# Shifting the on-chip addresses of the normalised activations by 32 bytes and of every other tile by 256 bytes

## The chip, the core and the metric

The kernel runs on one core of one Trainium2 chip. The metric is the device time of one launch in microseconds, as the median of three runs. "PE" is TensorE, "DVE" VectorE, "ACT" ScalarE, "POOL" GpSimd and "SP" SyncE, which issues the DMAs. SBUF is the on-chip memory of 128 partitions; an address below is a byte offset within a partition.

## The reference, cut to what matters

One sequence of 256 tokens with 1024 features goes through two layers of a first block and one layer of a second. Each layer multiplies normalised activations by large weight matrices:

```python
for l in range(2):                                  # first block
    h = rmsnorm(x, norm_mix[l])
    proj = h @ w_in[l]                              # 1024 x 5956
    ...
    x = x + merged @ w_out[l]
    h = rmsnorm(x, norm_ffn[l])
    g, u = jnp.split(h @ w_ffn_in[l], 2, axis=-1)   # 1024 x 5632
    x = x + (jax.nn.silu(g) * u) @ w_ffn_out[l]     # 2816 x 1024
...                                                 # second block: the same shape of work, once
h = rms_norm(x, mix_pre_g) * (1.0 + sc1) + sh1
y = hybrid_mixer(h, w_in, ...)
x = x + g1 * rms_norm(y, mix_post_g)
h = rms_norm(x, ffn_pre_g) * (1.0 + sc2) + sh2
y = swiglu_ffn(h, w_ffn_in, w_ffn_out)
```

All of it is float32.

## The kernel before, in words

**How a product is made.** Each float32 operand is split into a rounded part H and a remainder L (both of type fp32r), and a product is the sum of three matmuls, H·H, H·L and L·H (`mm3`, line 776). Weights come from HBM in 350 tiles of 128 partitions x 1024 columns (tag `raw`, 4 buffers); ACT writes the H half (`wH`) and DVE the L half (`wL`), 6 buffers each (`do_split`, line 716). The normalised activations of a stage are split in the same way into two tiles of 128 x 8 x 256, `xH` and `xL`, made by `act_pair` (line 868).

**What PE does with them.** Before each matmul, a load of weights (the profile's engine row PEld) brings a 128 x 128 block into the array; then the other operand, the moving one, streams through. In a name such as `mm<-xH,wL`, the first operand is the moving one and the second the loaded one. There are five kinds of fp32r matmul:

- `pair_mm` (line 781): moving `xH` or `xL`, 256 columns; loaded `wH` or `wL`. Called for the input projections, the gates and both halves of the first FFN product (`ffn`, lines 1360 and 1362).
- `proj_mm` (line 790): moving a `b4` tile (name `b` in the profile), 256 columns.
- `out_mm` (line 890): moving a `t512` tile (`t`) or an `E` tile, 256 columns.
- `token_mm` (line 799) and `first_tm` (line 1326): moving `wH` or `wL`, 512 columns; loaded `xH` or `xL`.
- `out_tm` (line 902): moving `wH` or `wL`, 512 columns; loaded `xH` and `xL` (where `act_pair` holds the mixer's output, line 1630) or a `t512` tile.

**What sets the order.** All instructions are recorded first (`Recorder`, line 346; the profile therefore gives nearly every instruction line 396) and then issued in an order that a list scheduler works out from fixed costs per instruction. The costs depend on shapes and engines, not on addresses.

**Where tiles lie.** `new` (line 640) makes tiles of a multiple of 128 bytes per partition, and the pools hand out addresses in the order in which tags are first used. In the built program `raw`, `wH`, `wL`, `xH`, `xL` and all `b4` tiles start at 256 bytes past a multiple of 512. All `t512` and `E` tiles start at 384 bytes past one. The slices that a matmul reads inside these tiles are 512, 1024 or 2048 bytes long and lie at multiples of 512 bytes from the tile's start, except slices of the two small weight tiles (68 and 8 columns).

Of the kernel before, what the change touches and what calls it, by code (L numbers as in the profile page):

```python
# [16 lines left out]
F32R = mybir.dt.float32r  # L17
# [9 lines left out]
LAST = 0.0  # L27
FF, NJ = 2816, 11
LINE = 128
OUT_SHAPE = [256, 1024]  # L30
EPS = 1e-6
NEG = -1e30
# [583 lines left out]
def program(tc, I, out, pw, cw, tap=None, stop=None):  # L616
# [11 lines left out]
    with es:  # L628
        es.enter_context(tc.manual_schedule())
        const = es.enter_context(tc.tile_pool(name="const", bufs=1))  # L630
        wp = es.enter_context(tc.tile_pool(name="wp", bufs=3))
        act = es.enter_context(tc.tile_pool(name="act", bufs=1))
# [4 lines left out]
        def body():  # L637
            uid = [0]

            def new(pool, shape, dt=F32, tag=None, bufs=None):  # L640
                n = int(np.prod(shape[1:]))
                line = LINE if dt == U8 else LINE // 4
                if pool is not psum and pool is not dram and n % line:

                    v = new(pool, [shape[0], -(-n // line) * line], dt, tag, bufs)[:, :n]
                    return v if len(shape) == 2 else v.rearrange("p (a b) -> p a b", a=shape[1])
                uid[0] += 1
                b = Buf(pool, shape, dt, f"{tag or 'c'}_{uid[0]}", tag, bufs or 1, "PSUM" if pool is psum else "SBUF")
                return View(b, np.arange(n).reshape([1] + list(shape[1:])), shape[0], ())
# [98 lines left out]
            DMA.dma_start(cst[:, :early], I["consts"][:, :early])  # L748
            DMA.dma_start(cst[:, early:], I["consts"][:, early:])
            msk = new(const, [128, 5, 32], U8)  # L750

            def load_masks():
                m = b4()[:, :160]
                DMA.dma_start(m, I["masks"])
                V.tensor_copy(msk.rearrange("p a b -> p (a b)"), m)
# [110 lines left out]
                return v, r, rstd  # L866

            def act_pair():
                return (new(act, [128, 8, 256], F32R, tag="xH", bufs=1), new(act, [128, 8, 256], F32R, tag="xL", bufs=1))

            def scaled_split(g, acc=None):

                H, L = act_pair()
                for c in range(8):
                    if acc is not None and c % 2 == 0:
                        tt(x2(c // 2), x2(c // 2), acc[c // 2], OP.add)
                    A(H[:, c], xT[:, c], AF.Copy, scale=g[:, c:c + 1])
                    stt(L[:, c], xT[:, c], g[:, c:c + 1], H[:, c].bitcast(F32), OP.mult, OP.subtract)
                return H, L
# [575 lines left out]
            for i, n in enumerate(("mix", "ffn")):  # L1455
                a = new(const, [128, 8])
                stt(a, mod[f"sc{i + 1}"], 1.0, P(f"{n}_pre_g"), OP.add, OP.mult)
                b = new(const, [128, 8])
# [3 lines left out]
            def modulated(n):  # L1462
                g, _, sh, _ = G[n]
                rstd = rstd_of(squares(x2), 1024, "side", True)[2]
                H, L = act_pair()
                for p in range(4):
                    t = t512()
                    tt(v2(t), xT[:, 2 * p:2 * p + 2], bc(rstd, 2), OP.mult)
                    for b in range(2):
                        c = 2 * p + b  # L1470
                        s = slice(b * 256, b * 256 + 256)
                        if c in MOD_V:
                            ts(t[:, s], t[:, s], g[:, c:c + 1], sh[:, c:c + 1], OP.mult, OP.add)
                        else:
                            A(t[:, s], t[:, s], AF.Identity, scale=g[:, c:c + 1], bias=sh[:, c:c + 1])
                    w = lambda ap: ap[:, 2 * p:2 * p + 2].rearrange("p a b -> p (a b)")
                    split_into(w(H), w(L), t)
                return H, L
# [39 lines left out]
            def modulated_tm(n):  # L1518
                g, _, sh, _ = G[n]
                H, L = act_pair()  # L1520
                first = first_tm()
                for t in range(2):
                    R.bias = EARLY if t == 0 else 0.0
                    r = inv_rms(lambda h: xt[:, t, h * 512:h * 512 + 512])
                    for h in range(2):
                        z, m, ps = t512(), t512(), bank()
                        ts(z, xt[:, t, h * 512:h * 512 + 512], r, 32.0, OP.mult, OP.mult)
                        for i in range(4):
                            PE.transpose(ps[:, i * 128:i * 128 + 128], z[:, i * 128:i * 128 + 128], ident)
                        for i in range(4):  # L1530
                            c = 4 * h + i
                            sl = slice(i * 128, i * 128 + 128)
                            if i < ON_V[h]:
                                ts(m[:, sl], ps[:, sl], g[:, c:c + 1], sh[:, c:c + 1], OP.mult, OP.add)
                            else:
                                A(m[:, sl], ps[:, sl], AF.Identity, scale=g[:, c:c + 1], bias=sh[:, c:c + 1])
                        w = lambda ap: ap[:, 4 * h:4 * h + 4, t * 128:t * 128 + 128]
                        split_into(w(H), w(L), m.rearrange("p (a b) -> p a b", a=4))
                    R.bias = 0.0
                    pend = first(t, H, L)  # L1540
                return (H, L), pend
# [4 lines left out]
            for tag, n in (("iq", 16), ("AT1", 16), ("cr", 8), ("sr", 8), ("qnc", 8), ("qns", 8), ("knc", 8), ("kns", 8)):  # L1546
                n = min(n, 16 * GROUPS - len(taps))
                if n > 0:
                    t = new(act, [128, n, 32], F32, tag=tag)
# [137 lines left out]
            post("ffn", ffn(X, None, None, out_tm, first), True)  # L1687

        body()
        R.issue()  # L1690
        tc.predicted = R.predicted
# [16 lines left out]
```

## Time and profile before

| | |
|---|---|
| median of 3 runs | 1154.72 us (1154.36 to 1154.79) |
| the profiled execution | 1152.33 us |
| its span, first to last instruction | 1150.6 us |
| PE busy | 1120.6 us (97%), 9388 matmuls |
| DVE busy | 857.8 us (75%) |
| ACT busy | 595.1 us (52%) |
| DMA queue of the weights | 55.6% of 16 engines' time |
| mean granted TensorE clock | 0.995 of full speed |

The span is 1.7 us shorter than the device time of the same execution, and that execution is 2.4 us (0.2%) below the median. A matmul's busy time in the profile is its latency, so the busy times of neighbours overlap; what one matmul costs in a stream is the distance from its start to the next start. The chain of waits gives that for whole streams: its pieces state how long a run of consecutive matmuls held the end of the program, and how many there were.

### The profile page before, as it was taken

The page shows a single profiled execution, that of the slowest core. Times are in us where ns is not written, and L with a number is a line of the kernel's source. Part 1 is how long each engine was busy: PE and PEld are TensorE (multiplying, and loading weights), DVE is VectorE, ACT ScalarE, POOL GpSimd, SP SyncE. Part 2 cuts the span into 40 slices and gives each one's busy share as a digit, 9 for nine tenths or more (in the row PEclk, how much of TensorE's full clock was granted, in tenths as well). Part 3 has the DMA queues.
Part 4 walks back from the last instruction along what each step waited for, and adds up shares of the span by engine and source line. Part 5 has one row for each costly group of instructions (what it writes and reads, how often), then busy time and mean ns, then how long its engine had stood idle before and what let it go on. Part 6 is the DMA issues. An engine that isn't in the chain of part 4 may idle for free.

```text
span 1150.6 us, 22970 instructions
## 1 busy us (share of the span) xinstructions
PE 1120.6 (97%) x9388; PEld 1060.2 (92%) x9388; DVE 857.8 (75%) x1590; ACT 595.1 (52%) x905; POOL 7.2 (1%) x16
## 2 busy tenths in 40 slices
PE   6999999999999999999999999999899989999996
PEld 6989999999999999888999999999799568999995
DVE  7999976889965589998676998755879668444554
ACT  6745594544444467446745544444654665443442
POOL 1000000000000000000000000000000000000000
PEclk9999999999999999999999999999999999999999
DMA  7553544788956543644355898656456325556550
GB/s 268 173 188 107 185 131 155 245 283 327 334 170 216 185 146 113 218 133 135 133 177 189 287 347 310 209 195 194 137 173 182 107 74 196 169 177 209 184 165 36
DMA packets 59992, 217.47 MB, mean 189 GB/s; under 512 B 6872, under 2 KB 10096, under 8 KB 56816
## 3 DMA queue, kind: packets, MB, share of 16 engines
q1 hardware_dynamic: 59888, 216.02, 55.6%
q8 instruction: 73, 1.20, 0.4%
q14 instruction: 31, 0.25, 0.1%
HBM read 214.19 MB, written 1.63 MB: 188 GB/s over the span
## 4 chain that ended last, share of the span: by engine, by line
PE 95%; DVE 2%; ACT 1%; issue 1%; DMA 0%; SPq 0%; DVEq 0%; ACTq 0%
PE mm L396 66%; PE side L396 29%; DVE small L396 1%; DVE b L396 1%; DVE wL L396 0%; DMA raw<-in_W 0%; ACT t L396 0%; ACT wH L396 0%; DVE t L396 0%; DVE xL L396 0%; SPq L396 0%; DVE E L396 0%; DVE c L396 0%; DVE AC L396 0%; DVEq L1704 0%
## 5 line engine op out<-in xcount | busy, mean ns | idle before, releaser
L396 ACT ACTIVATE wH<-raw 128x1024 fp32r<-128x1024 f32 (+1 forms) x390 | 368.6, 967 | 420.6 <-PE mm L396 227.0
L396 DVE TENSOR_TENSOR wL<-raw,wH 128x1024 fp32r<-128x1024 f32 (+1 forms) x390 | 425.0, 1110 | 163.6 <-ACT wH L396 162.0
L396 PE MATMUL mm<-xH,wH 128*128 128x256 f32 x1760 | 497.0, 285 | 9.2 <-ACT wH L396 9.2
L396 PE MATMUL mm<-xL,wH 128*128 128x256 f32 x1760 | 499.3, 285 | 0.5 <-DVE xL L396 0.5
L396 PE MATMUL mm<-xH,wL 128*128 128x256 f32 x1760 | 499.3, 286 | 0.3 <-DVE wL L396 0.3
L396 PEld LDWEIGHTS mm<-xH,wH 128*128 128x128 f32 x1760 | 336.4, 192 | 11.6 <-ACT wH L396 9.2
L396 PEld LDWEIGHTS mm<-xL,wH 128*128 128x128 f32 x1760 | 337.2, 192 | 3.3 <-issue 0.9
L396 PEld LDWEIGHTS mm<-xH,wL 128*128 128x128 f32 x1760 | 336.7, 192 | 2.8 <-DVE wL L396 1.0
L396 PE MATMUL side<-t,wH 128*128 128x256 f32 x704 | 128.0, 282 | 0.0
L396 PEld LDWEIGHTS side<-t,wH 128*128 128x128 f32 x704 | 108.7, 189 | 0.0
L396 PE MATMUL side<-t,wL 128*128 128x256 f32 x352 | 99.1, 281 | 0.0
L396 ACT ACTIVATE t<-t 128x512 f32<-128x512 f32 (+2 forms) x80 | 48.8, 618 | 42.5 <-DVE t L396 40.0
L396 PEld LDWEIGHTS side<-t,wL 128*128 128x128 f32 x352 | 66.3, 188 | 0.0
L396 DVE SCALAR_TENSOR_TENSOR E<-E,b 128x1024 f32<-128x1024 f32 x48 | 57.9, 1218 | 6.1 <-DMA E<-in_ada 6.1
L396 PE MATMUL side<-wH,t 128*128 128x512 f32 x176 | 57.3, 394 | 0.0
L396 DVE TENSOR_TENSOR t<-t,t 128x512 f32<-128x512 f32 (+2 forms) x78 | 53.0, 679 | 3.9 <-ACT t L396 2.9
L396 DVE TENSOR_TENSOR t<-mm,rstd 128x512 f32<-128x512 f32 (+1 forms) x50 | 33.9, 677 | 18.9 <-PE mm L396 18.7
L396 PE MATMUL mm<-b,wH 128*128 128x256 f32 x256 | 46.7, 283 | 0.0
L396 PE MATMUL side<-E,wH 128*128 128x256 f32 x256 | 46.4, 282 | 0.0
L396 PE MATMUL mm<-wH,xH 128*128 128x512 f32 x96 | 38.3, 407 | 2.3 <-ACT xH L396 2.3
L396 PEld LDWEIGHTS mm<-b,wH 128*128 128x128 f32 x256 | 39.9, 192 | 0.0
L396 PEld LDWEIGHTS side<-E,wH 128*128 128x128 f32 x256 | 39.4, 188 | 0.0
(205 smaller groups left out, 1195.0 us busy)
## 6 DMA issues: line engine op xcount, KB each, us to landing
raw<-in_W SPq DMA_DIRECT2D x348, 512.0 KB, 4.3
E<-in_ada SPq DMA_DIRECT2D x24, 1024.0 KB, 7.3
b<-c SPq DMA_DIRECT2D x16, 128.0 KB, 3.9
c<-in_xT SPq DMA_DIRECT2D x4, 256.0 KB, 4.5
raw<-in_W SPq DMA_DIRECT2D x4, 256.0 KB, 3.8
b<-in_c SPq DMA_DIRECT2D x2, 512.0 KB
out_y<-E SPq DMA_DIRECT2D x4, 256.0 KB, 2.0
c<-E SPq DMA_DIRECT2D x4, 143.0 KB, 3.5
```

Of the source, the lines that this page charges most:

```text
L396: op.emit = lambda: getattr(real, method)(*[get(a) for a in args], **{k: get(a) for k, a in kw.items()})
```

## The change

Two things are moved in SBUF, and nothing else is touched. A tile of 64 float32 (256 bytes) that no instruction uses is allocated ahead of all others, so that every tile starts 256 bytes later. The two tiles of `act_pair` become 512 bytes longer (2048 + 128 elements), and the activations begin 8 elements (32 bytes) into them; what lies behind them moves by a further 1024 bytes in all.

```diff
+GAP = 64
+
+PLACE = 8
...
             msk = new(const, [128, 5, 32], U8)
+            new(const, [128, GAP]).real()
...
             def act_pair():
-                return (new(act, [128, 8, 256], F32R, tag="xH", bufs=1), new(act, [128, 8, 256], F32R, tag="xL", bufs=1))
+                return tuple(new(act, [128, 2048 + 128], F32R, tag=t, bufs=1)[:, PLACE:PLACE + 2048].rearrange("p (a b) -> p a b", a=8)
+                             for t in ("xH", "xL"))
```

On every engine the same instructions stand in the same order, with the same waits, in the programs built from both. The start addresses in the built programs, as bytes past a multiple of 512:

| data | before | changed |
|---|---|---|
| `raw`, `wH`, `wL`, `b4` | 256 | 0 |
| `xH`, `xL` (the activations themselves) | 256 | 32 |
| `t512`, `E` | 384 | 128 |
| moving minus loaded: `pair_mm` (x against w) | 0 | 32 |
| moving minus loaded: `proj_mm` (b against w) | 0 | 0 |
| moving minus loaded: `out_mm` (t or E against w) | 128 | 128 |
| moving minus loaded: `token_mm`, `first_tm`, first `out_tm` (w against x) | 0 | -32 |
| moving minus loaded: `out_tm` in the last FFN (w against t) | -128 | -128 |

## Rows read from the trace of the kernel before

**Rows 1.** The page: span, busy times, granted clock, chain by engine.
```profile
span 1150.6 us, 22970 instructions
...
PE 1120.6 (97%) x9388; PEld 1060.2 (92%) x9388; DVE 857.8 (75%) x1590; ACT 595.1 (52%) x905; POOL 7.2 (1%) x16
...
PEclk9999999999999999999999999999999999999999
...
PE 95%; DVE 2%; ACT 1%; issue 1%; DMA 0%; SPq 0%; DVEq 0%; ACTq 0%
```
**Rows 2.** Instruction groups of PE: busy, mean ns | idle before, releaser.
```profile
L396 PE MATMUL mm<-xH,wH 128*128 128x256 f32 x1760 | 497.0, 285 | 9.2 <-ACT wH L396 9.2
L396 PE MATMUL mm<-xL,wH 128*128 128x256 f32 x1760 | 499.3, 285 | 0.5 <-DVE xL L396 0.5
L396 PE MATMUL mm<-xH,wL 128*128 128x256 f32 x1760 | 499.3, 286 | 0.3 <-DVE wL L396 0.3
L396 PE MATMUL side<-t,wH 128*128 128x256 f32 x704 | 128.0, 282 | 0.0
L396 PE MATMUL mm<-wH,xH 128*128 128x512 f32 x96 | 38.3, 407 | 2.3 <-ACT xH L396 2.3
L396 PE MATMUL side<-wH,xH 128*128 128x512 f32 x32 | 12.8, 401 | 0.8 <-DVE b L396 0.8
```
**Rows 3.** Chain of waits, PE pieces: start us, length us, what, how many.
```profile
392.15 10.55 PE mm L396 x88
568.73 28.43 PE mm L396 x237
```
**Rows 4.** The same view, pieces of out_mm with moving E tiles.
```profile
211.78 12.24 PE side L396 x103
616.59 14.02 PE side L396 x118
```
**Rows 5.** Timeline of PE, proj_mm, first and last of 96 matmuls: start us, us.
```profile
172.43 0.40 PE L396 MATMUL mm<-b,wH 128*128 128x256 f32 x2
...
183.83 0.28 PE L396 MATMUL mm<-b,wL 128*128 128x256 f32 x1
```
**Rows 6.** Timeline of PE, out_tm loading xH and xL, 18 matmuls apart.
```profile
937.75 0.39 PE L396 MATMUL side<-wL,xH 128*128 128x512 f32 x1
...
941.83 0.39 PE L396 MATMUL side<-wL,xH 128*128 128x512 f32 x1
```
**Rows 7.** Chain of waits, out_tm in the last FFN, loading t512 tiles.
```profile
1131.69 7.92 PE side L396 x34
```
**Rows 8.** Timeline of PE where only 8 columns are loaded, five steps.
```profile
830.13 0.39 PE L396 MATMUL mm<-xH,b 128*8 128x256 f32 x2
...
830.69 0.33 PE L396 MATMUL mm<-xL,wH 128*128 128x256 f32 x1
```
**Rows 9.** Busy time by stretch: PE, PEld, DVE, ACT, POOL, clock, DMA, GB/s.
```profile
225.00:411.00 186.00, 185.82 (x1556) 185.82 (x1557) 138.46 (x179) 82.40 (x93) 0.00 (x0) 1.00 0.71 250
631.00:826.00 195.00, 193.84 (x1623) 193.19 (x1621) 147.65 (x210) 91.98 (x114) 0.00 (x0) 1.00 0.71 245
950.00:1140.00 190.00, 189.30 (x1281) 175.15 (x1282) 99.00 (x121) 81.39 (x105) 0.00 (x0) 0.99 0.51 167
```
**Rows 10.** Groups that make the activations and split weights; last, DMA to landing.
```profile
L396 ACT ACTIVATE xH<-c,c 128x256 fp32r<-128x256 f32 x32 | 14.6, 496 | 4.2 <-DVE c L396 2.8 <-DMA c<-in_xT 1.4
L396 DVE SCALAR_TENSOR_TENSOR xL<-c,c,xH 128x256 fp32r<-128x256 f32 x32 | 14.2, 478 | 2.1 <-ACT xH L396 2.1
L396 DVE TENSOR_TENSOR wL<-raw,wH 128x1024 fp32r<-128x1024 f32 (+1 forms) x390 | 425.0, 1110 | 163.6 <-ACT wH L396 162.0
raw<-in_W SPq DMA_DIRECT2D x348, 512.0 KB, 4.3
```

## The prediction

> **What bounds the kernel now.** I read the page first, then the chain of waits, then PE's timeline inside the streams that the chain names. The page shows PE busy for 97% of a span of 1150.6 us at the full granted clock, and a chain that runs through PE for 95% of the time [rows 1]. So whatever one matmul of a long stream costs is paid at the end of the program, as long as the engines that feed it keep up. The groups show which streams there are: three groups of 1760 matmuls with moving `xH` or `xL` make 5280 of 9388, with hardly 10 us of idle time ahead of them [rows 2]. The mean of 285 ns there is a latency, and neighbours overlap. The price of one matmul comes from the chain: 88 of them in 10.55 us and 237 in 28.43 us, or 119.9 and 120.0 ns each [rows 3].
>
> The reader should now set that beside streams of the same shape whose operands lie elsewhere. Matmuls of 256 columns whose moving tile is an `E` tile cost 12.24 us / 103 = 118.8 ns, and 14.02 us / 118 = 118.8 ns in another stage [rows 4]. Those with a moving `b4` tile start at 172.43 and 183.83 us with 95 steps between them: 120.0 ns [rows 5]. In the first and last of these three the moving operand starts at the same place as the loaded one, modulo 512 bytes; in the `E` stream it starts 128 bytes further. With 512 moving columns the order is the other way round: 18 steps in 4.08 us, 226.7 ns, where both start at the same place [rows 6], and 7.92 us / 34 = 232.9 ns where the loaded tile is 128 bytes ahead of the moving one [rows 7]. So the distance between the two operands is worth 1 to 6 ns per matmul in this very trace, though which distance is good can't be read off from two of them.
>
> One more reading bears on it. 120.0, 226.7 and the 112 ns of the stretch where only 8 columns are loaded (0.56 us over five steps [rows 8], read to 10 ns, so 110 to 114) lie close to 18, 34 and 17 times 6.67 ns. As an estimate from these rows alone, a stream at distance 0 repeats on a grid of 6.67 ns: what a pair of load and matmul needs is rounded up to the next rung. The `E` stream, at 118.8, isn't on a rung, so it pays only what it needs.
>
> **The change part by part.** No instruction is added or removed, and no queue or wait is reordered; only addresses differ.
>
> *Everything 256 bytes further.* Distances between `w`, `b4`, `t512` and `E` tiles stay what they were. If only distance counts, the streams of rows 4, 5 and 7 keep their price. I take zero. If the absolute place modulo 512 counts as well, each of the 1440 matmuls of `out_mm` (704 of them in one group [rows 2]) could go from 118.8 to the 120.0 of the other streams, or the 384 of `proj_mm` the other way: +1.7 or -0.5 us. Those are the ends.
>
> *DMAs and the vector engines.* The weight tiles land 256 bytes further, and landing takes 4.3 us at the median with the DMA queue at 55.6%; I cost it at nothing, since the splits wait on buffers that PE frees and the four `raw` buffers cover the landing. ACT's and DVE's writes of `xH` and `xL`, 32 of 496 ns and 32 of 478 ns [rows 10], go to addresses 32 bytes off. If each took a tenth longer, 32 x 0.1 us = 3 us would be added to both engines, most of it beside PE; I take zero. What covers these is DVE's slack: it is busy for 74%, 76% and 52% of the three FFN stretches [rows 9]. PE's time there would have to shrink by a quarter before DVE set the pace.
>
> *`pair_mm` at distance 32 instead of 0: 5280 matmuls.* The trace before has no stream at this distance. Below, it is bounded by the rung of rows 8, 17 x 6.67 = 113.3 ns: -6.7 x 5280 = -35 us. Above, by the next rung, 19 x 6.67 = 126.7 ns: +6.7 x 5280 = +35 us. The nearest row is the `E` stream: same shape, a moving operand that also starts behind the loaded one, and 118.8 ns off the grid [rows 4]. I take it: (118.8 - 119.9) x 5280 = -5.8 us.
>
> *`token_mm`, `first_tm` and the first `out_tm` at distance -32: 384 matmuls* (three times 96 and three times 32 [rows 2]). Here the loaded operand starts ahead. The rows bound it by 226.7 and 232.9 ns [rows 6, 7]: 0 to +2.4 us. I take the middle, +1.2 us, since 32 bytes lies between 0 and 128.
>
> The sum is -5.8 + 1.2 = -4.6 us. The profiled execution took 1152.33 us, so it would take 1147.7; the median of the runs is 2.4 us above that execution, and the forecast for it is 1154.72 - 4.6 = **1150.1 us**.
>
> [...] The row shows 120.0 ns at one distance and 118.8 at another [rows 3, 4]. [...]
>
> **The rivals.**
>
> *Nothing changes: 1154.7 us.* The stream stays on the 120.0 rung, because 32 bytes removes too little of what a pair needs, or because rows 4 and 5 differ for another reason: the `E` stream also writes to other PSUM banks and changes its moving slice every third matmul. For it: the `b4` and `x` streams agree to 0.1 ns although one is `proj_mm` and the other `pair_mm`. Against it: in the 512-column streams the function is `out_tm` in both cases, and rows 6 and 7 still differ. Chance 0.22.
>
> *The stream falls to the next rung down: about 1120 us.* Most of the 1.2 ns would not be the point then, but the rounding: if distance 32 frees 6.7 ns, the stream repeats at 113.3 ns. That is -35 us. For it speaks that such a price occurs at all for 256 columns [rows 8]; against it that only 8 columns were loaded there, so most of the load's own cost was missing. Chance 0.15, any result below 1135 us included.
>
> *Slower, by one mechanism: the pair needs more than 120.0 ns and is rounded up.* [...] If every pair is rounded up, it is +35 us, 1190 us. If the stream leaves the grid and averages 1 to 2 ns above 120, it is +5 to +10 us, 1160 to 1165 us. For it: the 512-column rows lose 6.2 ns by leaving distance 0 [rows 6, 7]. Against it: at 256 columns, which is 14 times as many matmuls here, leaving it gained. Chance 0.27, of which 0.16 lies below 1165 us.
>
> **How the numbers follow.** The forecast's own case has 0.36: 1145 to 1152 us. About 0.2% (2.3 us) is what a measurement of this kernel can tell from no change. Faster by more than that is my case and the lower rung, 0.36 + 0.15 = 0.51; within it 0.22; slower 0.27. The likeliest case has a bit over a third, so the range has to reach to the others: from 1130 us, which takes in half of a fall to the lower rung in part of the stages, to 1164 us, which takes in the mild loss. Left out are a full fall (0.09) and the higher rung (0.11).
>
> **What would show it.** In the changed profile the chain's `mm` pieces of the FFN stretches should cost 118 to 119 ns per matmul instead of 119.9, and no longer a constant number in the timeline; the `side` pieces of rows 4 should stay at 118.8 and `proj_mm` at 120.0; the 512-column stretch of rows 6 should lie between 226.7 and 232.9. Durations on ACT and DVE should be the same to 1%. I am wrong if the `x` streams repeat at exactly 120.0 (no change), 113.3 or 126.7 ns (rungs), or if streams whose distances stay the same change their price, which would mean that the absolute place counts.

## The result, and the profile after

The change makes the kernel faster: 1142.16 us as the median of four runs (1141.65 to 1142.53), against 1154.76 us for the kernel before in the same comparison (four runs, 1154.36 to 1156.05). The ratio is 0.9889, 95% interval 0.9872 to 0.9906. The profiled execution took 1142.15 us; the one of before took 1152.33 us, so between the two traces there are 10.2 us to find, and 12.6 us between the medians. The missing 2.4 us are the distance of the earlier profiled execution from its own median. Part of it goes with the clock: that execution had a mean granted clock of 0.995, and in the comparisons below the kernel before took 1152.4 to 1153.4 us where the clock was 0.995 and 1155.0 to 1155.2 us where it was 0.988.

The page of the changed kernel, the lines that answer to [rows 1]:

```profile
span 1140.3 us, 22970 instructions
...
PE 1109.3 (97%) x9388; PEld 1046.7 (92%) x9388; DVE 857.7 (75%) x1590; ACT 595.2 (52%) x905; POOL 7.2 (1%) x16
...
PE 92%; DVE 3%; ACT 2%; DMA 1%; issue 1%; SPq 0%; DVEq 0%; ACTq 0%
```

PE is still the bound. DVE and ACT are as busy as before to 0.1 us; PE is busy for 11.3 us less, with the same number of matmuls. The chain of waits shows where, in the pieces that answer to [rows 3, 4, 7] (start us, length us, what, how many):

```profile
388.28 10.27 PE mm L400 x88
...
563.60 28.16 PE mm L400 x237
...
210.82 12.24 PE side L400 x103
...
611.09 14.02 PE side L400 x118
...
1121.48 7.91 PE side L400 x34
```

The 88 matmuls of the FFN's first product went from 10.55 to 10.27 us, so from 119.9 to 116.7 ns each. The long piece of 237 moved less, 28.43 to 28.16 us, because 144 of its matmuls are `proj_mm`, whose operands kept their distance, and only 91 move x. The two pieces with moving `E` tiles kept their length, 12.24 and 14.02 us, and so did the last piece, 7.92 and 7.91 us.

The 512-column matmuls that load `xH` and `xL` went the other way. In PE's timeline of the first `out_tm` (start us, length us), 15 steps take 3.50 us, 233.3 ns each, where [rows 6] gave 226.7:

```profile
931.00 0.40 PE L400 MATMUL side<-wL,xH 128*128 128x512 f32 x1
...
934.50 0.40 PE L400 MATMUL side<-wL,xH 128*128 128x512 f32 x1
```

From here on, the **price** of a stream is the mean distance from one matmul's start to the next start of the same kind, worked out from all start times in a trace and leaving out steps over 140 ns (260 ns for 512 columns), which are waits or lie at the low granted clock described below. The table has the prices and, in the last two columns, all distances from a start to the next added up, waits included:

| matmuls | count | before, ns | after, ns | before, us | after, us |
|---|---|---|---|---|---|
| 256 columns, moving x | 5280 | 119.73 | 116.83 | 650.0 | 636.7 |
| 256 columns, moving `b` | 384 | 119.85 | 119.73 | 46.0 | 46.0 |
| 256 columns, moving `E` or `t` | 1440 | 118.78 | 118.55 | 171.0 | 170.7 |
| 512 columns, loading x | 384 | 228.3 | 233.1 | 92.8 | 95.6 |
| 512 columns, loading `t` | 264 | 232.1 | 232.4 | 61.1 | 61.2 |
| all others | | | | 110.3 | 111.5 |

So 13.3 us came from `pair_mm`: 14.0 us inside its streams and 0.5 us where they pass to other matmuls, less 1.1 us by which the waits grew.

The 512-column matmuls that load x gave back 2.8 us. Their price accounts for 1.8 us of that (4.8 ns x 384). The rest goes with the clock: behind a stretch in which PE was mostly idle (busy for 1.12 of 3.40 us from 946.8 us on before, for 1.46 of 3.50 us from 934.1 us on after) the granted clock was 0.50 in place of 1.00, for 3.4 us before (from 950.2 us on) and for 10.2 us after (from 937.6 us on), and 7 of these matmuls started in it before, 13 after. That isn't due to their distance. In `gap_only` (below), with all distances as before, 12 started at this clock and the sum is 93.9 us; in `place_only` (below), with the distances of the change, 8 did and it is 94.6.

The 1.2 us of the remaining matmuls can't be told from no effect, since kernels with equal distances differ by as much (110.2 us in `gap_only`, 111.4 in `p256`). Unrounded, the differences add up to 9.7 us; of the other 0.6 us of the span's 10.3, 0.5 lie ahead of the first matmul.

The streams of `E`, `t` and `b` kept their distances and yet cost 0.1 to 0.3 ns less (`t` 118.51 ns against 118.78). The place isn't the reason: in `gap_only` they cost what they did before, in `place_only` what they do after the change. What changed beside them are the x streams.

### The profile page after: what moved, and what is told of

Read it like the earlier page. It is cut to its first block, busy times and chain, and to the rows that moved or that the text cites. A ratio compares the mean times of both kernels' runs of the same rounds, so it can differ in the third digit from the quotient of the medians.

```text
span 1140.3 us, 22970 instructions
## 1 busy us (share of the span) xinstructions
PE 1109.3 (97%) x9388; PEld 1046.7 (92%) x9388; DVE 857.7 (75%) x1590; ACT 595.2 (52%) x905; POOL 7.2 (1%) x16
## 4 chain that ended last, share of the span: by engine, by line
PE 92%; DVE 3%; ACT 2%; DMA 1%; issue 1%; SPq 0%; DVEq 0%; ACTq 0%
PE mm L400 63%; PE side L400 29%; ACT t L400 1%; DMA raw<-in_W 1%; DVE wL L400 1%; DVE t L400 1%; DVE small L400 1%; ACT wH L400 0%; ACT L604 0%; DVE b L400 0%; SPq L400 0%; DVE xL L400 0%; DVE E L400 0%; DVEq L1710 0%; ACT xH L400 0%
## 5 line engine op out<-in xcount | busy, mean ns | idle before, releaser
L400 DVE TENSOR_TENSOR wL<-raw,wH 128x1024 fp32r<-128x1024 f32 (+1 forms) x390 | 425.5, 1112 | 156.1 <-ACT wH L400 154.0
L400 PE MATMUL mm<-xH,wH 128*128 128x256 f32 x1760 | 490.9, 281 | 8.7 <-ACT wH L400 8.7
L400 PE MATMUL mm<-xH,wL 128*128 128x256 f32 x1760 | 493.0, 282 | 0.7 <-DVE wL L400 0.7
L400 PE MATMUL mm<-xL,wH 128*128 128x256 f32 x1760 | 493.0, 282 | 0.5 <-DVE xL L400 0.5
L400 PEld LDWEIGHTS mm<-xH,wH 128*128 128x128 f32 x1760 | 330.4, 189 | 11.1 <-ACT wH L400 8.7
L400 PEld LDWEIGHTS mm<-xL,wH 128*128 128x128 f32 x1760 | 331.3, 189 | 3.5 <-issue 0.9
L400 PEld LDWEIGHTS mm<-xH,wL 128*128 128x128 f32 x1760 | 330.7, 188 | 3.4 <-DVE wL L400 1.6
```

What stands on the lines that cost most here:

```text
L400: op.emit = lambda: getattr(real, method)(*[get(a) for a in args], **{k: get(a) for k, a in kw.items()})
```

## The experiments

The theory at this point: only the distance between the moving and the loaded operand counts, and 32 bytes has another price than 128. The rivals: the place modulo 512 counts; or any distance but 0 does the same. All the kernels below have the same instructions in the same order as the change. Where a kernel was run only once, the price in its trace is the evidence and the time goes along without an interval.

### The two halves of the change

```diff
 gap_only:    -PLACE = 8
              +PLACE = 0
 place_only:  -            new(const, [128, GAP]).real()
```

> Only the 256-byte gap, activations at the start of their tiles: all distances as before, all places 256 bytes further. Distance theory: x streams at 120.0 ns per 256-column matmul, 512-column ones that load x at 226.7 ns, time 1154.7 us within 0.2%. Rival, place modulo 512 counts: x streams below 118.5 ns, time below 1150 us.

> Only the 32 bytes inside the x tiles, no gap: x at 288 and weights at 256 past a multiple of 512. Distance theory: as the full change, x streams 116.8 ns and 512-column ones that load x 233 ns, time 1142 us within 3 us. Rival, the weights have to start at a multiple of 512: x streams stay at 119 to 120 ns, time 1150 to 1155 us.

The gap alone: 1153.41 us, ratio 0.9998 (0.9989 to 1.0007), x at 119.73 ns, every other price within 0.1 ns of before. The shift alone: 1141.37 us, ratio 0.9893 (0.9879 to 0.9908), x at 116.83 ns, 512 columns loading x at 233.2. The gap does nothing that these runs can tell; the 32 bytes are the whole change. The place modulo 512 is ruled out as the cause of the gain.

### The distance of the `E` stream, and the other sign

```diff
-PLACE = 8
 p128:  +PLACE = 32
 p480:  +PLACE = 120
```

> Gap kept, activations 128 bytes into their tiles: the distance of the E stream. Distance theory: x streams at 118.7 ns as the E stream (what the forecast took for 32 bytes), 512-column ones that load x at 232 ns, time 1149 to 1152 us. Rival, any distance but 0 does the same: 116.8 ns and 1142 us.

> Gap kept, activations 480 bytes into their tiles, so the loaded weights start 32 bytes ahead of the moving x, modulo 512, and in token_mm, first_tm and the first out_tm the moving operand is 32 ahead. If only the size of the distance counts: as the change, x streams 116.8 ns, 1142 us. If the sign counts, as the 512-column rows suggest: x streams at 120 or above, 1155 us or more, and the 512-column matmuls that load x below 230 ns.

At 128 bytes: 1150.91 us, ratio 0.9977 (0.9967 to 0.9986). The x stream costs 118.82 ns and the 512-column one 232.4 ns, against 118.77 for the moving `E` tiles and 232.4 for the 512-column matmuls that load `t` in the same trace. So [rows 4] did tell the price at 128 bytes, for x as well, and the rival "any distance does the same" falls. At 480 bytes: 1148.35 us, ratio 0.9957 (0.9942 to 0.9972), x at 118.32 ns. The sign counts: 32 bytes ahead and 32 bytes behind differ by 1.5 ns. But my expectation for that case, 120 ns or more, was wrong, and so was the one for the 512-column matmuls: they cost 233.2 ns at +32 bytes, as at -32. For these, every distance tried so far but 0 costs about the same (192 bytes, below, is an exception with 229.7 ns).

### The curve from 16 to 256 bytes, and the other operand moved

```diff
-PLACE = 8
 p16:   +PLACE = 4
 p64:   +PLACE = 16
 p256:  +PLACE = 64
 w224, instead of the gap of 64 elements one of 120, not rounded up; PLACE = 8 stays:
-            new(const, [128, GAP]).real()
+            View(Buf(const, [128, 120], F32, 'gap', None, 1, 'SBUF'), np.arange(120).reshape(1, 120), 128, ()).real()
```

> Gap kept, activations 16 bytes into their tiles. If half the shift does part of it, x streams between 116.8 and 120.0 ns and a time of 1142 to 1154 us; if what helps is to be off the grid by any amount, 116.8 ns or below and 1142 us.

> Gap kept, activations 64 bytes into their tiles. If the price grows steadily from 32 bytes (116.8 ns) to 128 (118.8), x streams at about 117.5 ns, 1145 us; if 64 bytes is a whole step of the memory and so the same as distance 0, 120.0 ns and 1154 us.

> Gap kept, activations 256 bytes into their tiles, the farthest from distance 0 modulo 512. If only closeness to 0 counts, x streams at 118.8 ns or below; if the price repeats every 256 bytes, 120.0 ns and 1154 us.

> Same distance as the change but the other operand moved: the gap is 480 bytes, so weights start at 224 and x at 256 past a multiple of 512. Distance theory: x streams 116.8 ns, 512-column ones that load x 233 ns, 1142 us within 3 us. Rival, it is x that must start off a larger block: x streams at 119 to 120 ns, 1150 us or more.

A single run each, of 16, 64, 256 and 224 bytes: 1140.17, 1142.95, 1154.25 and 1141.68 us. With weights at 224 and x at 256 bytes the x price is 116.85 ns, as in the change, so it doesn't matter which operand starts off a round address; the rival falls. 256 bytes is the same as 0: 119.74 ns, and the chain's piece of 88 has its old length. That piece in the chains of three kernels (start us, length us, what, how many), first at 256, then at 128, then at 64 bytes:

```profile
392.27 10.55 PE mm L400 x88
```
```profile
390.88 10.44 PE mm L400 x88
```
```profile
389.00 10.37 PE mm L400 x88
```

That is 119.9, 118.6 and 117.8 ns. So 256 bytes cost what 0 bytes do, 119.74 and 119.73 ns, as the second case of the expectation had it; that the price repeats every 256 bytes is shown for this one pair of distances alone.

### A step of 4 bytes, 192 bytes, and the other streams moved too

```diff
 p4:    PLACE = 1
 p192:  PLACE = 48
 all32 (x16_all32 has PLACE = 4 besides):
-            def act_pair():
-                return tuple(new(act, [128, 2048 + 128], F32R, tag=t, bufs=1)[:, PLACE:PLACE + 2048].rearrange("p (a b) -> p a b", a=8)
-                             for t in ("xH", "xL"))
+            def act_pair(place=PLACE):
+                pair = []
+                for t, n in (("xH", 2048 + 128), ("xL", 2048 + 128 + PLACE)):
...
+                    v = View(Buf(act, [128, n], F32R, f"{t}_{uid[0]}", t, 1, "SBUF"), np.arange(n).reshape(1, n), 128, ())
+                    pair.append(v[:, place:place + 2048].rearrange("p (a b) -> p a b", a=8))
+                return tuple(pair)
...
-                rq8 = new(act, [128, 2, 8], F32, tag="rq8")
+                rq8 = new(act, [128, 128], F32, tag="rq8")[:, :16].rearrange("p (a b) -> p a b", a=2)
...
-            mH, mL = act_pair()
+            mH, mL = act_pair(0)
```

> As the change, and the b4, E and t512 tiles moved as well, so that every moving operand of 256 columns starts 32 bytes past the loaded one; the mixer's output pair, which is only loaded, starts at the beginning of its tiles (distance 0 again for 96 of the 384 matmuls of 512 columns). Distance theory: 384 matmuls with b from 119.8 to 116.8 ns, 1440 with t or E from 118.6 to 116.8, 96 from 233 to 227: 1.2 + 2.6 + 0.6 = 4.4 us below the change, 1137 to 1139 us. Rival, these streams are set by what they are (PSUM banks, order of slices): 1141 to 1143 us.

> As all32, but the activations themselves 16 bytes into their tiles. From the look at 16 bytes (116.7 ns): within 1 us of all32, 1136 to 1139 us; if the 2 us that the 16-byte look was below the change are real, 1135 to 1137 us.

> As the change with activations 4 bytes into their tiles. If any step off distance 0 is enough: x streams about 116.8 ns, 1140 to 1143 us. If operands must start at 16 bytes: x streams above 120 ns, 1155 us or more. If 4 bytes is too small to count: 119.7 ns, 1154 us.

> As the change with activations 192 bytes into their tiles, which is 64 bytes ahead for the loaded operand if the price repeats every 256 bytes. Between the 118.8 ns of 128 and the 118.3 ns of 480 bytes: 118 to 119 ns, 1148 to 1151 us.

The longer `xL` tile moves what is allocated behind it, `b4` first, to 32 bytes; the 384 bytes more in `rq8` bring `E` and `t512` there too. With every moving operand at 32 bytes: 1137.29 us, ratio 0.986 (0.9844 to 0.9877). `b` costs 116.69, `E` 116.63 and `t` 116.66 ns, as x does at this distance. Here the streams follow the distance, whatever they hold and wherever they write. The version with x at 16 bytes gave 1138.75 us (ratio 0.9874, 0.9859 to 0.9889); the two intervals overlap, so the advantage of 16 bytes that the single run seemed to show isn't confirmed, and the x price was 117.59 ns here and 116.70 there.

4 bytes: 1171.59 us, slower than before by 18 us, x at 123.02 ns. That is the second of the three cases, but its reason isn't shown: 4 bytes is the only distance tried for x that isn't a multiple of 16, so the distance may cost this, or a start off such a multiple. 192 bytes missed its expectation: 1130.86 us where 1148 to 1151 was expected, x at 114.55 ns. The same piece of the chain, 4 bytes first, then 192:

```profile
398.13 10.83 PE mm L400 x88
```
```profile
385.28 10.01 PE mm L400 x88
```

These are 123.1 and 113.8 ns. So the price doesn't grow steadily with the distance in either direction, and a shift of 4 bytes is worse than none.

### How narrow the dip is, which load counts, and everything at 192 bytes

```diff
 all192: as all32 with PLACE = 48 and rq8 of 64 elements
 p160:   PLACE = 40
 p208:   PLACE = 52
 wl4:    PLACE = 48, and
-                L = new(wp, [128, 1024], F32R, tag="wL", bufs=N_SPLIT)
+                L = new(wp, [128, 1088], F32R, tag="wL", bufs=N_SPLIT)[:, 47:1071]
```

> As all32 with 192 bytes in place of 32. If the streams with b, E and t follow the same curve: x streams 114.6 ns, b from 119.7 to 114.6 (384 of them, 2.0 us), E and t from 118.9 to 114.6 (1440, 6.2 us), 512-column ones that load t from 232.1 to 229.7 (0.6 us): 1121 to 1124 us. Rival, 192 bytes is good for x alone: 1130 us.

> As the change with activations 160 bytes into their tiles. If the price falls steadily from 118.8 ns at 128 to 114.6 at 192: 116 to 117.5 ns, 1136 to 1144 us; if 192 is a dip by itself, 118 ns or above, 1147 us or more.

> As the change with activations 208 bytes into their tiles. If the price climbs steadily from 114.6 ns at 192 to 118.3 at 224 (the run at 480): 115.5 to 117.5 ns, 1134 to 1143 us; if 192 is a dip by itself, 118 ns or above.

> As the 192-byte run, but the L halves of the weights 188 bytes into tiles that are 256 bytes longer: the distance of x to wH stays 192, to wL it is 4, which cost 123 ns where it held throughout. In each group of three (xH by wH, xL by wH, xH by wL) the second streams while wL is loaded for the third. If the next load counts, the second is the long one, by 4 ns or more; if the load that a matmul itself uses counts, the third. The mean of the three lies between 114.6 and 123 ns either way, and the time between 1131 and 1172 us.

160 and 208 bytes: 1148.42 and 1151.31 us, x at 118.12 and 118.83 ns. In the mean over all streams 192 bytes is a narrow dip; both steady curves fall.

The run with `wL` at another distance gave 1147.54 us (the other streams that use `wL` have another distance to it as well, so the time isn't x alone). In the trace of before, the load of `wL` for the third of a group of three starts at 393.90 us, where the second starts to stream (393.90), 0.12 us ahead of the third itself. In the group of three, the first cost 117.36 ns, the second 116.86 and the third 119.86 (1618, 1630 and 1611 pairs). The third is the long one, so it is rather the load that a matmul itself uses; but it is longer by 2.5 to 3.0 ns and not by the 4 or more that I had asked for, and how much of a late start carries over to the next matmul isn't shown. I leave it open.

Everything at 192 bytes: 1133.19 us, ratio 0.9808 (0.9792 to 0.9825), ten microseconds short of the expectation. `b` and `E` came to 115.54 ns, `t` only to 117.78, and the x streams, whose distance is that of the 192-byte run, cost 116.10 ns in place of 114.55. The chain shows why the mean is misleading. Two neighbouring stages of the last FFN in this one trace:

```profile
1001.24 10.00 PE mm L400 x88
...
1017.43 10.37 PE mm L400 x88
```

The same stream, at the same distance, runs at 113.6 ns in one stage and at 117.8 in the next. At this distance it has two patterns that repeat: of the steps in unbroken stretches of 25 x steps or more, 1486 lie in stretches with a mean near 113.5 ns and 2557 in stretches with a mean near 117.8, and only 40 in between.

### The version that beats both

```diff
 x192_all32, on all32:
-            def act_pair(place=PLACE):
+            def act_pair(place=48):
 p192_again: p192 unchanged
```

> The 192-byte kernel once more, timed. If a stream at one distance has one price: 1130 to 1132 us in all runs. If it can settle in more than one pattern, as the x streams of the version with everything at 192 suggest: runs spread from 1130 to 1139 us.

> x at 192 bytes, b4, E and t512 at 32. If the prices add up: x streams 114.6 ns as in the 192-byte run, b at 116.7 and E and t at 116.7 as in all32, 3.8 us below it: 1126 to 1128 us. If the pattern of a stream depends on the phase in which the one before leaves it: x streams 115.5 ns or more, 1131 us or more.

The 192-byte kernel, timed: 1130.32 us (1129.98 to 1131.4), ratio 0.9798 (0.9784 to 0.9811), x at 114.58 ns. The time is steady, as the first case of the expectation has it, but the streams aren't. Counted in the same way, 763 of 4089 steps in the trace of `p192` and 745 of 4065 in this one lie in stretches near 117.8 ns, and they aren't all the same stretches. Here is one piece of the chain, first from `p192`, then from this run of the same program on another chip:

```profile
160.10 26.34 PE mm L400 x223
```
```profile
160.39 25.94 PE mm L400 x223
```

Its longest x stretch, 90 steps, took 117.8 ns a step in the first and 113.5 in the second. So the addresses and the order of the instructions alone don't fix the pattern; what does, no run here shows.

With the other streams at 32 bytes: **1124.03 us** (1121.61 to 1124.54), ratio **0.9737** (0.9724 to 0.975), 18 us below the change. The expectation of 1126 to 1128 was even exceeded: x costs 113.87 ns, because nearly all of its streams settle in the short pattern (4006 of 4034 steps, counted as above; why they do here isn't shown), and `b`, `E` and `t` cost 116.7 to 116.8. Its chain, to be set beside the pieces of the result's section:

```profile
208.92 12.03 PE side L400 x103
...
383.00 9.99 PE mm L400 x88
...
603.12 13.78 PE side L400 x118
```

All prices of the x stream over the distance modulo 256 bytes, from the traces of all these kernels (224 is the run at 480 bytes). The last row goes behind the mean: the levels, in ns, near which the means of single stretches of 25 or more x steps lie, in the trace of one kernel for each distance.

| bytes | 0 | 4 | 16 | 32 | 64 | 128 | 160 | 192 | 208 | 224 |
|---|---|---|---|---|---|---|---|---|---|---|
| mean, ns | 119.73 | 123.02 | 116.70 | 116.83 | 117.34 | 118.82 | 118.12 | 114.55 | 118.83 | 118.32 |
| levels | 119.8 | 123.1 | 113.3, 116.7, 118.7 | 116.7, 117.8 | 113.3, 117.8 | 118.7, 120.0 | 117.4, 118.7 | 113.6, 117.8 | 116.7, 119.1 | 118.3 |

So the row of means is no smooth curve: much the same levels come back at different distances, and a mean says how many steps took which. At 16 bytes 977 of 4068 steps lay at the lowest level in the single run and 136 of 4095 in `x16_all32`, hence 116.70 and 117.59 ns. The order of 16, 32 and 64 bytes in the row of means is therefore not shown.

## Why the prediction was right in direction and wrong in size

**What bounds the kernel: right.** The streams of PE set the end: the x steps got 13.3 us shorter in sum and the span 10.3, with the rest accounted for above, and the chain still runs through PE for 92% (95% before). DVE's slack held: `wL` took 1112 ns in the mean against 1110 [rows 10], and its cover of a quarter wasn't needed for 1% less.

**Everything 256 bytes further, at zero: right.** `gap_only` measured 0.9998.

**DMAs and the vector engines, at zero: right.** `xH` took 496 ns before and after, `xL` 482 against 478 ns, and the median landing 4.2 us against 4.3.

**`pair_mm`, -5.8 us: this is the term that failed.** The step reads "The nearest row is the `E` stream: same shape ... I take it". It took the price at 128 bytes for the price at 32, -1.1 ns a matmul where -2.9 was measured. The `p128` run shows that the row had been read rightly, since x costs 118.82 ns at that distance and the kernel then gains 0.2%; and that it was the row of another distance, since at 32 bytes x costs 116.83. In the trace the term is -13.3 us. The first half of the mechanism stood: the stream left the 120.0 ns and its steps are no longer constant. The second half, that a stream off the grid "pays only what it needs" and so has one price, didn't: streams settle at one of a few levels, 116.7 and 117.8 ns at 32 bytes, 118.7 and 120.0 at 128. What was missing is that nothing in the trace of before said how the price goes between two distances, and in the means it doesn't go steadily: 123.0 ns at 4 bytes, 116.7 at 16, 114.6 at 192, 118.8 at 208. The bounds I had named, 113.3 and 126.7 ns, held all of these; the choice inside them went by likeness alone.

**The 384 matmuls that load x, +1.2 us: the right sign, too small.** I took the middle between 226.7 and 232.9 ns because 32 lies between 0 and 128. There was no such middle: 233 ns with x at 32, 64 and 480 bytes, a little above the bound of 232.9 that [rows 7] gave, 232.4 at 128, 229.7 at 192, 228.4 at 256. The price rose by 4.8 ns, so the term is +1.8 us; the sum of their steps grew by 2.8 us, the rest of it by the clock, as said above.

The sum, -4.6 us, stands against -10.2 us between the two traces and -12.6 us between the medians. The forecast of 1150.1 us was 7.9 us too high. The time lies inside the range, but by the range's width: 1142.2 us falls between the forecast's own case (1145 to 1152 us) and the lower rung (below 1135), where no case had been described.

**The rivals.** "Nothing changes" didn't happen. Its objection that the `E` stream might differ for its PSUM banks or its order of slices is answered by `all32`, where moving the tiles moved those prices as well, and by `p128`. That the distance matters is shown by the x prices from 113.9 to 123.0 ns of these runs; by what mechanism, they don't show. "The next rung down" was not reached at 32 bytes but is what 192 bytes does: 113 and 114 ns make up 3692 of 4992 steps there, 113.3 in the mean. The argument against it, that at 8 columns most of the load's own cost is missing, was an estimate: in the trace of before a load of 8 columns for moving `xH` is busy for 103 ns in the mean, one of 128 columns for 192. "Slower" didn't happen at 32 bytes, but it does at 4: x costs 123.02 ns and the kernel takes 1171.59 us. That its mechanism, rounding up, is at work there isn't shown: all steps but one lie between 116 and 126 ns, below the rung of 126.7.

## What to carry to other kernels

Where a stream of matmuls bounds a kernel, try the distance between the moving tile and the loaded tile, modulo 256 bytes, as a parameter of its own: here it is worth 2.6% without touching an instruction. Sweep it on the chip, in steps of 16 bytes and in the whole kernel, and read the price from the chain's pieces of equal count; neither neighbouring distances nor a stream at another distance predict it (116.83 ns at 32 bytes, 123.02 at 4, 118.82 at 128). Look at single stretches besides the mean, since a good price can be lost from one stage to the next (113.6 and 117.8 ns at 192 bytes) and from one execution to the next (117.8 and 113.5 ns). Leave the operands of 512-column matmuls at equal places if these are many: they cost 228.3 ns there (228.4 at 256 bytes) and 229.7 to 233.2 at 32, 64, 128, 192 and 480 bytes.

## What the runs showed of the hardware that I had not expected

- The price of a 256-column fp32r matmul in a stream goes from 113.9 to 123.0 ns with the addresses of its two operands alone, at a mean granted clock of 0.995 (`x192_all32`) and 0.991 (`p4`), and is the same at 256 bytes as at 0 (119.74 and 119.73 ns).
- At distance 0 most steps are constant: 4316 of 4991 x steps of the kernel before are 120 ns. The starts of its 64 unbroken stretches of 20 or more such steps (moving x or `b`), counted from the trace's own zero and taken modulo 20/3 ns (6.67), leave nearly the same remainder: 5.0 ns at 60 us, falling to between 3.0 and 3.3 ns at 1100 us with a scatter of some tenths (4.0 at 392 us, 4.7 at 473), across all the idle gaps between. That fits a grid of about 6.67 ns that no stream begins anew, an estimate from these remainders; what would keep it, no run here shows.
- Off distance 0 a stream can repeat in more than one pattern (10.00 and 10.37 us for the same 88 matmuls in neighbouring stages; 117.8 and 113.5 ns for the same 90 steps in two executions of one program), so a distance alone doesn't fix a price.
- Why the distance between the two operands has a price, and whether it is the one to the matmul's own load or to the next one, isn't settled. A load of the x streams is busy for 188 to 189 ns in the mean in the changed kernel, longer than the 117 ns from one matmul to the next.
